# Loads ahead, stores issued by ACT, and a first chunk without a state, in a one-core hybrid decoder layer

## The chip, the core and the metric

The kernel runs on one core of a Trainium2 chip, in one launch. The metric is the device time of an execution in microseconds (us), as the median of several runs. The core has five engines that each work through their own list of instructions in order and wait for one another by semaphores: PE (TensorE, matrix multiplies), DVE (VectorE, elementwise), ACT (ScalarE, activations, copies and casts), POOL (GpSimd) and SP (SyncE, which here issues every DMA). SBUF is the on-chip memory with 128 partitions, PSUM holds the results of matmuls in banks of 128 x 512 float32, and DRAM is the memory outside. A tile is a buffer in SBUF or PSUM. A tile pool gives each tag a fixed number of buffers, and a tile that needs a buffer waits until its last user is done. The names of engines with a q behind them (SPq) are their DMA issues.

## The reference

One decoder layer over 2048 tokens of width 1024, in float32. A normalised input goes through one projection into two head groups. Group A is a Mamba-2 scan over 16 heads of 64 in chunks of 128 tokens, with a causal convolution ahead and a gated norm behind. Group B is a short gated convolution. Both are put side by side, projected back, normalised and added; a gated embedding follows. Cut to what matters here:

```python
def ssd_chunked(x, dt, a, b_mat, c_mat, d_skip):
    ...
    a_cs = jnp.cumsum(adt, axis=-1)
    decay_in = jnp.exp(segsum(adt))
    cb = jnp.einsum("bclgn,bcsgn->bgcls", cc, bc)
    y_diag = jnp.einsum("bgrcls,bcsgrp->bclgrp", cb[:, :, None] * decay_in, xd)
    ...
    states = jnp.einsum("bclgn,bclgrp->bcgrpn", bc, xd * decay_states[..., None])
    init = jnp.zeros_like(states[:, :1])
    states = jnp.concatenate([init, states], axis=1)
    ...
    y_off = jnp.einsum("bclgn,bcgrpn->bclgrp", cc, prev_states) * decay_out[..., None]
    y = (y_diag + y_off).reshape(bsz, length, SSD_HEADS, p)
    return y + d_skip[:, None] * x

def hybrid_layer(...):
    h = rmsnorm(x, norm_pre)
    proj = h @ w_in
    ...
    y_ssd = ssd_chunked(xs, dt, a, bm, cm, d_skip).reshape(bsz, length, D_MIX_SSD)
    yz = (y_ssd * jax.nn.silu(z_ssd)).reshape(bsz, length, SSD_GROUPS, D_MIX_SSD // SSD_GROUPS)
    y_ssd = rmsnorm(yz, ssd_norm.reshape(SSD_GROUPS, -1)).reshape(bsz, length, D_MIX_SSD)
    v = causal_dwconv(sc_c * sc_h, sc_conv_w)
    y_sc = sc_b * v * jax.nn.silu(z_sc)
    mix = jnp.concatenate([y_ssd, y_sc], axis=-1) @ w_out
    x = x + rmsnorm(mix, norm_post)
    gate = jax.nn.sigmoid(x @ w_ple_gate)
    return x + gate * (p_i @ w_ple_proj)
```

## The kernel before

The layout is transposed: features lie on the partitions, tokens run along the row. Tokens come in two halves of 1024 (index b) and four groups of 512 (index tg). Each big matrix product is made from float32 operands that were split into a high and a low part: ACT casts the high part, DVE subtracts to get the low part, and PE runs three passes (`PASSES`, L219). `split_w` (L145) does this for weights, `split_act` (L212) for activations. Weights come from one list through six buffers (`Weights`, L118); a weight is loaded and split, or it was split before, stored in DRAM and is loaded ready (`stored`, L152).

Stage A is the input projection. It takes both halves one after the other, with a Winograd-like scheme of seven products in place of eight (`Wino`). Products of column groups `gc`, `gb` (short convolution), `xs`, `z`, `cb` (scan) follow `order_` (L347). During the second half `later_weights` (L537) splits weights of later stages between the products: first those of the embedding's gate (`loads`, `sg_d`), then the lower rows of the output projection, in sixteen pieces A_o that are loaded into four buffers (tag h2), split by `keep` and stored to `so_d`. The results of stage A (xs_d, gz_d, cb_d, acs_d, ysc_d) go to DRAM.

The heads' stage puts two works side by side on PE. `under` (L894) multiplies the short convolution's part of the output projection (matmuls os, 256 units of three passes); each bank is copied by ACT to po (L918) and stored to part_d by SP (L919). Between the units runs the scan as a list of steps: for each half b four pairs j of head groups. PE's order is fixed as it is written (`InOrder`, L807). The other engines' order is made by the compiler's scheduler, which simulates the program and lets instructions run ahead of the written order. In a pair, `loads` brings xs, `mask_load` the four rows m from acs_d (four buffers), `transposes` makes xd and xdd, `decays` and `mask` run the exponentials on ACT (L1003, L1040) and the masks on DVE (L1043). `states` multiplies (pst), walks the chunks on DVE (L1027, into sprev, with the last state kept in carry for the next half) and scales ea (L1030). `offsets` multiplies the state of each chunk with ea (py from ea and sprev), `outputs` adds the inner products (py from m and xd), then DVE forms the rows (L1071, L1072), SP stores them to yz_d (L1073), ACT squares them (L1075, L1077) and DVE sums the squares (L1078, ssum). After the four pairs `inv_rms` (L236) makes the norm: PE sums over partitions (pn), ACT copies, SP stores to and loads from grs_d, ACT and DVE make the inverse root.

Normalised rows for the output projection are made by `mixes` (L883): `mix_load` loads pairs of rows into the three buffers of pool pld (class `Loads`, L832), `mix_pair` scales (L872) and splits them. The unit counter in `under` takes one entry of the list `new` per unit, in the first half only at every second unit.

Stage three, `out_proj` (L1155), multiplies the heads' part of the output projection (mo, L226) and adds the stored partial sums part (L1180) into tiles x (tag x2, 36 buffers), with ACT's squares behind; `norm` and `residual` add the input xres (L1210, L1213). `gate_seven` (L1240) multiplies for the gate (mg). The pool pl3 holds the loads of part and xres in three buffers. `second(tg, ..., lag)` (L1293) says how many units ahead the residual's loads begin. The pools of this stage take the memory of the heads' pools t4 and per, so a tile there waits for the last user of what lay there.

Of the kernel before, what the change touches and what calls it, by code (L numbers as in the profile page):

```python
# [7 lines left out]
F32 = mybir.dt.float32  # L8
# [56 lines left out]
def hybrid_kernel(ctx: ExitStack, tc: tile.TileContext, xT, pT, w_t, w_dt, w_o, w_g, w_p, cols_d, cst_d, outT):  # L65
# [303 lines left out]
    with ExitStack() as st:  # L369
# [167 lines left out]
        def later_weights():  # L537
# [24 lines left out]
            for d in range(KD):  # L562
                for q in range(2):
                    w = A.ph.tile([P, TG], F32, tag="h2", name=f"A_o{d}_{q}")
                    nc.sync.dma_start(w.rearrange("p (k c) -> p k c", c=P), w_o[d, :, 4 * (q + 2):4 * (q + 2) + 4, :])
                    keep(so_d[d][q], w, f"A_os{d}_{q}")
                    yield
# [314 lines left out]
    L = Loads(ctx, "pld", 3)  # L882
    def mixes(tg, k0):  # L883
# [5 lines left out]
    with ExitStack() as st:  # L889
        t4 = st.enter_context(tc.tile_pool(name="t4", bufs=2))  # L890
        per = st.enter_context(tc.tile_pool(name="per", bufs=1))
        carry = per.tile([P, 4, P], F32, name="carry")

        def under():  # L894


            new, unit = [], 0
# [40 lines left out]
        def heads(b):  # L938
# [3 lines left out]
            def begin():  # L942
                s["ct"] = per.tile([P, TB], F32, tag="ct", name=f"ct_{b}")
# [3 lines left out]
                s["gsb"] = [per.tile([P, TB], F32, tag=f"gsb{gr}", name=f"gsb_{b}{gr}") for gr in range(2)]  # L947
                s["btok"] = per.tile([P, NCH, P], F32, tag="btok", name=f"btok_{b}")
# [24 lines left out]
            def pair(j):  # L973
# [35 lines left out]
                def states():  # L1009
# [5 lines left out]
                    sp_ = st["sp"] = t4.tile([P, NCH, P], F32, tag="sprev", name=f"sprev_{b}{j}", bufs=1)  # L1015
                    ea = st["ea"]
                    if b == 0:
                        G.memset(sp_[:, 0, :], 0.0)
                    else:
                        G.tensor_copy(sp_[:, 0, :], carry[:, j, :])  # L1020
                    for c in range(NCH):
                        if c == NCH - 1 and b == NB - 1:
                            break
                        dstn = sp_[:, c + 1, :] if c + 1 < NCH else carry[:, j, :]
                        for hh in range(2):
                            hs = slice(64 * hh, 64 * hh + 64)
                            V.scalar_tensor_tensor(dstn[:, hs], sp_[:, c, hs], ea[:, hh, (c + 1) * CH - 1:(c + 1) * CH],  # L1027
# [17 lines left out]
                def offsets():  # L1045
# [3 lines left out]
                    for c in range(NCH):  # L1049
# [349 lines left out]
```

## Time and profile before

| What | us |
|---|---|
| median of 3 runs | 1663.52 |
| lowest and highest run | 1659.56, 1663.94 |
| profiled execution | 1660.71 |
| its span, first to last instruction | 1659.0 |
| DVE busy | 1273.4 |
| ACT busy | 805.7 |
| POOL busy | 69.3 |

The profile is of one execution. Its span is the time from the first to the last instruction; 1.7 us of the execution lie outside it. Busy time of an engine leaves out its semaphore and DMA-issuing instructions. Stage A ends at about 1031 us, the heads' stage at about 1306 us, the output projection at about 1496 us of the span. In a time line a row gives the start and the length in us, engine, line, operation, the tile written and the tiles read, the shape and how many instructions were merged; in square brackets stand the idle time ahead of it and what ended it.

### The profile page before, as it was taken

The page shows a single profiled execution, that of the slowest core. Times are in us where ns is not written, and L with a number is a line of the kernel's source. Part 1 is how long each engine was busy: PE and PEld are TensorE (multiplying, and loading weights), DVE is VectorE, ACT ScalarE, POOL GpSimd, SP SyncE. Part 2 cuts the span into 40 slices and gives each one's busy share as a digit, 9 for nine tenths or more (in the row PEclk, how much of TensorE's full clock was granted, in tenths as well). Part 3 has the DMA queues.
Part 4 walks back from the last instruction along what each step waited for, and adds up shares of the span by engine and source line. Part 5 has one row for each costly group of instructions (what it writes and reads, how often), then busy time and mean ns, then how long its engine had stood idle before and what let it go on. Part 6 is the DMA issues. An engine that isn't in the chain of part 4 may idle for free.

```text
span 1659.0 us, 22821 instructions
## 1 busy us (share of the span) xinstructions
PE 1634.0 (98%) x8296; PEld 1344.2 (81%) x8296; DVE 1273.4 (77%) x1913; ACT 805.7 (49%) x1450; POOL 69.3 (4%) x79
## 2 busy tenths in 40 slices
PE   9999999999999999999999999999999999999998
PEld 8888888888888888788888888888788788888776
DVE  6998777987769999877768678478777747687785
ACT  8663444434337555543435345466667424234342
POOL 0000000000000311000000001000100000000000
PEclk9999999999999999999999999999999999999999
DMA  9352322774216478951323227788788635547996
GB/s 324 140 197 83 101 94 82 258 242 142 72 64 219 178 269 283 298 172 64 108 64 107 71 66 266 254 303 292 278 288 293 202 113 180 160 160 253 323 309 218
DMA packets 135557, 314.73 MB, mean 190 GB/s; under 512 B 18698, under 2 KB 20234, under 8 KB 135444
## 3 DMA queue, kind: packets, MB, share of 16 engines
q1 hardware_dynamic: 135444, 313.27, 55.3%
q8 instruction: 65, 1.06, 0.3%
q14 instruction: 48, 0.39, 0.1%
HBM read 221.81 MB, written 91.41 MB: 189 GB/s over the span
## 4 chain that ended last, share of the span: by engine, by line
PE 74%; DVE 10%; DMA 9%; ACT 4%; issue 2%; SPq 0%; DVEq 0%; ACTq 0%
PE mo L226 10%; PE mg_X L1278 4%; PE mg_Y L1278 4%; PE os L817 3%; PE A_ple L226 2%; DMA m<-acs_d 2%; ACT m L1040 1%; PE A_xs1X L322 1%; PE A_gc6X L322 1%; PE A_gb7X L322 1%; PE A_gb5X L322 1%; PE A_gc7X L322 1%; PE A_z3X L322 1%; PE A_xs3X L322 1%; PE A_gb6X L322 1%
## 5 line engine op out<-in xcount | busy, mean ns | idle before, releaser
L817 PE MATMUL os<-act_m,ws_os 128*128 128x512 f32 x768 | 184.6, 397 | 0.7 <-ACT A_z L749 0.7
L226 PE MATMUL mo<-act_m,ws_o 128*128 128x512 f32 x768 | 179.3, 394 | 3.5 <-DVE x L1180 3.3
L226 PEld LDWEIGHTS mo<-act_m,ws_o 128*128 128x128 f32 x768 | 144.0, 189 | 37.8 <-DVE x L1180 6.0
L817 PEld LDWEIGHTS os<-act_m,ws_os 128*128 128x128 f32 x768 | 142.9, 189 | 34.6 <-issue 4.2
L1278 PE MATMUL mg_X<-act_x2s,ws_g 128*128 128x512 f32 x384 | 90.8, 393 | 0.7 <-ACT gth L1249 0.7
L147 DVE TENSOR_TENSOR ws_A_gb<-wr_A_gb,ws_A_gb 128x512 fp32r<-128x512 f32 x96 | 65.7, 684 | 27.1 <-ACT ws_A_gb L146 27.1
L1278 PEld LDWEIGHTS mg_X<-act_x2s,ws_g 128*128 128x128 f32 x384 | 70.8, 188 | 18.6 <-ACT gth L1249 1.7
L146 ACT CAST ws_A_gc<-wr_A_gc 128x512 fp32r<-128x512 f32 x96 | 59.7, 622 | 49.7 <-PE A_gc5X L322 8.3
L146 ACT CAST ws_A_gb<-wr_A_gb 128x512 fp32r<-128x512 f32 x96 | 59.7, 622 | 48.4 <-issue 5.0
L668 DVE SCALAR_TENSOR_TENSOR xo<-ux,cols,xo 128x1024 f32<-128x1024 f32 x60 | 76.6, 1280 | 5.3 <-ACT xo L664 4.2
L1040 ACT ACTIVATE m<-m,adt 128x128 f32<-128x128 f32 x256 | 79.8, 390 | 0.5
L147 DVE TENSOR_TENSOR ws_A_gc<-wr_A_gc,ws_A_gc 128x512 fp32r<-128x512 f32 x96 | 65.8, 685 | 12.2 <-ACT ws_A_gc L146 11.4
L1278 PE MATMUL mg_Y<-act_x2s,ws_g 128*128 128x512 f32 x288 | 68.1, 392 | 1.7 <-DVE kp L1251 1.2
L1278 PEld LDWEIGHTS mg_Y<-act_x2s,ws_g 128*128 128x128 f32 x288 | 53.5, 188 | 14.7 <-DVE kp L1251 2.4
L1043 DVE SCALAR_TENSOR_TENSOR m<-m,gsb 128x1024 f32<-128x1024 f32 x32 | 39.5, 1247 | 28.2 <-ACT m L1040 20.0
L1180 DVE TENSOR_TENSOR x<-mo,part 128x512 f32<-128x512 f32 x32 | 22.1, 689 | 47.4 <-PE mo L226 42.4
L1185 ACT ACTIVATE sq<-x 128x512 f32<-128x512 f32 x28 | 17.7, 633 | 70.5 <-DVE x L1180 70.4
L146 ACT CAST ws_A_z<-wr_A_z 128x512 fp32r<-128x512 f32 x48 | 29.9, 623 | 40.9 <-DVE wr_A_z L199 13.9
L215 ACT CAST act_m<-mraw 128x512 fp32r<-128x512 f32 x64 | 37.5, 620 | 23.8 <-DMA mraw<-ysc_d 9.6
L146 ACT CAST ws_A_xs<-wr_A_xs 128x512 fp32r<-128x512 f32 x48 | 29.9, 623 | 36.6 <-issue 11.6
L226 PE MATMUL A_ple<-act_p,ws_p 128*128 128x512 f32 x192 | 45.8, 396 | 0.1
L147 DVE TENSOR_TENSOR ws_A_z<-wr_A_z,ws_A_z 128x512 fp32r<-128x512 f32 x48 | 32.9, 685 | 16.6 <-ACT ws_A_z L146 16.5
(521 smaller groups left out, 3742.7 us busy)
## 6 DMA issues: line engine op xcount, KB each, us to landing
ws_g<-sg_d SPq DMA_DIRECT2D x56, 512.0 KB, 5.0
wr_A_gc<-in_w_t_dram SPq DMA_DIRECT2D x64, 256.0 KB, 2.7
wr_A_gb<-in_w_t_dram SPq DMA_DIRECT2D x64, 256.0 KB, 3.0
ws_os<-so_d SPq DMA_DIRECT2D x32, 512.0 KB, 5.7
m<-acs_d SPq DMA_DIRECT2D x32, 512.0 KB, 6.4
sg_d<-A_gs SPq DMA_DIRECT2D x28, 512.0 KB, 4.3
ple_d<-A_pe SPq DMA_DIRECT2D x32, 256.0 KB, 3.9
wr_A_xs<-in_w_t_dram SPq DMA_DIRECT2D x32, 256.0 KB, 3.0
```

Of the source, the lines that this page charges most:

```text
L146: S.copy(sp[:, 0, :kn, :], raw[:, :kn, :])
L147: V.tensor_tensor(sp[:, 1, :kn, :], raw[:, :kn, :], sp[:, 0, :kn, :].bitcast(F32), ALU.subtract)
L215: S.copy(a[:, 0, :], src)
L226: TE.matmul(out, sp[:, a, (k0 + k) % 4, :], act[k0 + k][:, b, :], start=k0 + k == 0 and q == 0, stop=k0 + k == n - 1 and q == 2)
L322: TE.matmul(out, sp[:, a, k % 4, :], t[:, b, ts_], start=p in OPENS and k == 0 and q == 0, stop=k == nk - 1 and q == 2, skip_group_check=True)
L668: V.scalar_tensor_tensor(o, u[:, q:q + TB], col(w0 + q), o, ALU.mult, ALU.add)
L817: inst = f(*a, **k)
L1040: S.activation(m[:, c, :], m[:, c, :], AF.Exp, bias=nacs[b][:, h, c:c + 1])
L1043: V.scalar_tensor_tensor(mf, mf, 1.0, s["gsb"][gr], ALU.min, ALU.mult)
L1180: evac.append(V.tensor_tensor(x2[d], ps[:, i, :], pt[:, i, :], ALU.add))
L1185: S.activation(sq, x2[d], AF.Square)
L1278: TE.matmul(out, sp[:, a, k, :], ops_[t, p][k][:, b, :], start=p in OPENS and m_ == 0, stop=m_ == 11, skip_group_check=True)
```

## The change

- Stored halves: the sixteen pieces A_o are loaded three ahead of the piece that is split, in the written order. The four buffers stay.
- Rows ahead: for token group 2 the eight raw tiles of the short convolution are loaded one by one into pool praw (`load_raw`), from the last quarter of the first two groups' units on, and split one by one (`mix_tile`). The loads for groups 3 and 0 through pld are written earlier, and their splits are spread with empty entries (`no`).
- Stores: part_d and yz_d are stored by ACT (`S.dma_start`), the first right behind ACT's copy to po, the second behind ACT's square of the same tile.
- First chunk: the state ahead of chunk 0 is no longer cleared or copied into sprev by POOL. In the first half, chunk 0 has no product with a state, and chunk 1's state is a copy of pst. In the second half carry is read directly.
- Memory: ct, gsb and btok move to a new pool pg between t4 and per. In stage three the x tiles get a pool px of their own, then comes pl3, then the rest (pp).
- Residual loads for groups 2 and 3 begin 3 and 4 units ahead, in place of 2.

```diff
+            ahead = []
+            for n in range(2 * KD + 3):
+                if n < 2 * KD:
+                    d, q = divmod(n, 2)
+                    ahead.append(A.ph.tile([P, TG], F32, tag="h2", name=f"A_o{d}_{q}"))
+                    nc.sync.dma_start(ahead[n].rearrange("p (k c) -> p k c", c=P),
+                                      w_o[d, :, 4 * (q + 2):4 * (q + 2) + 4, :])
+                if n >= 3:
+                    d, q = divmod(n - 3, 2)
+                    keep(so_d[d][q], ahead[n - 3], f"A_os{d}_{q}")
                     yield
...
+    def mix_tile(raws, tg, k):
+        acts_o[tg][KD + k] = split_act(raws.pop(k), f"m_{tg}_{KD + k}", FIRST[2 * (tg % 2) + k // 4])
...
         t4 = st.enter_context(tc.tile_pool(name="t4", bufs=2))
+        pg_ = st.enter_context(tc.tile_pool(name="pg", bufs=1))
         per = st.enter_context(tc.tile_pool(name="per", bufs=1))
...
+            def load_raw(tg, k):
+                t = praw.tile([P, 4, P], F32, tag="wraw", name=f"mraw_{tg}_{KD + k}").rearrange("p k c -> p (k c)")
+                b, o = divmod(tg * TG, TB)
+                nc.sync.dma_start(t, ysc_d[b][k, :, o:o + TG])
+                raws[k] = t
...
+                    if dp == KD - 2:
+                        if t == 0:
+                            new += [lambda k=k: load_raw(2, k) for k in range(KD)]
+                        else:
+                            new += [no] * 10 + [lambda: mix_load(L, 0, 0), lambda: mix_load(L, 0, 2)]
...
                             S.copy(o, ps)
-                            nc.sync.dma_start(part_d[tg][dp + di], o)
+                            S.dma_start(part_d[tg][dp + di], o)
                         if dp == KD - 2 and tg < NG - 1:
-                            new += mixes(*((tg + 2, KD) if tg + 2 < NG else (tg + 2 - NG, 0)))
+                            ...
+                            if tg == 0:
+                                for k in range(KD):
+                                    new.append(lambda k=k: mix_tile(raws, 2, k))
+                                    if k in (2, 4, 6):
+                                        ld(3, KD + k - 2)()
+                            elif tg == 1:
+                                new += [mx(3, KD), ld(3, KD + 6), no, mx(3, KD + 2), no, mx(3, KD + 4), no, no, mx(3, KD + 6)]
+                            else:
+                                new += [mx(0, 0), ld(0, 4), no, mx(0, 2), ld(0, 6), no, no, no, mx(0, 4), no, no, mx(0, 6)]
...
-                    if b == 0:
-                        G.memset(sp_[:, 0, :], 0.0)
-                    else:
-                        G.tensor_copy(sp_[:, 0, :], carry[:, j, :])
+                    prev = st["prev"] = [carry[:, j, :] if b else None] + [sp_[:, c, :] for c in range(1, NCH)]
                     for c in range(NCH):
...
+                        if prev[c] is None:
+                            V.tensor_copy(dstn, pst[:, :P])
+                            continue
...
-                    for c in range(NCH):
+                    for c in range(0 if b else 1, NCH):
...
-                    nc.sync.dma_start(yz_d[b][jt], yv)
                     if j == 0:
                         S.activation(ssum, yv, AF.Square)
                     else:
                         S.activation(sq, yv, AF.Square)
                         V.tensor_tensor(ssum, ssum, sq, ALU.add)
+                    S.dma_start(yz_d[b][jt], yv)
...
+        px = st.enter_context(tc.tile_pool(name="px", bufs=NG * KD + 4))
+        L3 = Loads(st, "pl3", 3)
         pp = st.enter_context(tc.tile_pool(name="pp", bufs=2))
-        L3 = Loads(st, "pl3", 3)
...
-        second(2, 32, (40, 41, 43, 44), 2)
+        second(2, 32, (40, 41, 43, 44), 3)
...
-        second(3, 36, (56, 58, 60, 61), 2)
+        second(3, 36, (56, 58, 60, 61), 4)
```

More of the change, by code (lines that the diff above doesn't have):

```diff
@@ L561, in later_weights @@
                     yield
[L562 to L566, printed above, removed]
+            ahead = []
[8 more added lines that the diff above has]
+                    keep(so_d[d][q], ahead[n - 3], f"A_os{d}_{q}")
                     yield
@@ L890, in hybrid_kernel @@
         t4 = st.enter_context(tc.tile_pool(name="t4", bufs=2))
+        pg_ = st.enter_context(tc.tile_pool(name="pg", bufs=1))
         per = st.enter_context(tc.tile_pool(name="per", bufs=1))
         carry = per.tile([P, 4, P], F32, name="carry")
+        no = lambda: None
         def under():
-            new, unit = [], 0
+            new, unit, raws = [], 0, {}
+            def load_raw(tg, k):
[3 more added lines that the diff above has]
+                raws[k] = t
             for t in range(0, NG, 2):
@@ L942, in begin @@
             def begin():
-                s["ct"] = per.tile([P, TB], F32, tag="ct", name=f"ct_{b}")
+                s["ct"] = pg_.tile([P, TB], F32, tag="ct", name=f"ct_{b}")
                 nc.sync.dma_start(s["ct"], cb_d[b][0])
@@ L946, in begin @@
                 nc.sync.dma_start(s["bt"], cb_d[b][1])
-                s["gsb"] = [per.tile([P, TB], F32, tag=f"gsb{gr}", name=f"gsb_{b}{gr}") for gr in range(2)]
-                s["btok"] = per.tile([P, NCH, P], F32, tag="btok", name=f"btok_{b}")
+                s["gsb"] = [pg_.tile([P, TB], F32, tag=f"gsb{gr}", name=f"gsb_{b}{gr}") for gr in range(2)]
+                s["btok"] = pg_.tile([P, NCH, P], F32, tag="btok", name=f"btok_{b}")
                 s["ssum"] = [per.tile([P, TB], F32, tag=f"ssum{gr}", name=f"ssum_{b}{gr}") for gr in range(2)]
@@ L1014, in states @@
                                       s["btok"][:, c, 64 * gr:64 * gr + 64], xdd[gr][:, c, :], start=True, stop=True)
-                    sp_ = st["sp"] = t4.tile([P, NCH, P], F32, tag="sprev", name=f"sprev_{b}{j}", bufs=1)
+                    sp_ = t4.tile([P, NCH, P], F32, tag="sprev", name=f"sprev_{b}{j}", bufs=1)
                     ea = st["ea"]
-                    if b == 0:
-                        G.memset(sp_[:, 0, :], 0.0)
-                    else:
-                        G.tensor_copy(sp_[:, 0, :], carry[:, j, :])
+                    prev = st["prev"] = [carry[:, j, :] if b else None] + [sp_[:, c, :] for c in range(1, NCH)]
                     for c in range(NCH):
@@ L1023, in states @@
                             break
-                        dstn = sp_[:, c + 1, :] if c + 1 < NCH else carry[:, j, :]
+                        dstn = prev[c + 1] if c + 1 < NCH else carry[:, j, :]
+                        if prev[c] is None:
+                            V.tensor_copy(dstn, pst[:, :P])
+                            continue
                         for hh in range(2):
                             hs = slice(64 * hh, 64 * hh + 64)
-                            V.scalar_tensor_tensor(dstn[:, hs], sp_[:, c, hs], ea[:, hh, (c + 1) * CH - 1:(c + 1) * CH],
+                            V.scalar_tensor_tensor(dstn[:, hs], prev[c][:, hs], ea[:, hh, (c + 1) * CH - 1:(c + 1) * CH],
                                                    pst[:, c * P + 64 * hh:c * P + 64 * hh + 64], ALU.mult, ALU.add)
@@ L1056, in offsets @@
                                 bank[gr, c // 4, hh] = open_bank(f, TE.matmul(
-                                    st["py"][gr][hs, cs], st["sp"][rows, c, hs], st["ea"][rows, hh, cs], start=f is None,
+                                    st["py"][gr][hs, cs], st["prev"][c][rows, hs], st["ea"][rows, hh, cs], start=f is None,
                                     stop=False, skip_group_check=True))
@@ L1178, in out_proj @@
                     del sp[d]
-                x2[d] = pp.tile([P, TG], F32, tag="x2", name=f"x2_{tg}_{d}", bufs=NG * KD + 4)
+                x2[d] = px.tile([P, TG], F32, tag="x2", name=f"x2_{tg}_{d}")
                 evac.append(V.tensor_tensor(x2[d], ps[:, i, :], pt[:, i, :], ALU.add))
@@ L1215, in tmp @@
         def tmp(name):
-            return pp.tile([P, TG], F32, tag="x2", name=name, bufs=NG * KD + 4)
+            return px.tile([P, TG], F32, tag="x2", name=name)
         ops_, sums_ = {}, {}
```

3 lines of the change are left out of this document (2 added, 1 removed).

## The prediction

> **What bounds the kernel now.** I read the page first, then the waits of the tensor engine (PE), then the time lines of all engines around each of those waits.
>
> ```profile
> span 1659.0 us, 22821 instructions
> PE 1634.0 (98%) x8296; PEld 1344.2 (81%) x8296; DVE 1273.4 (77%) x1913; ACT 805.7 (49%) x1450; POOL 69.3 (4%) x79
> ```
>
> PE is busy for 1634.0 of 1659.0 us, and no other engine is over 81%. The kernel is bound by PE, so an edit can win only where PE waits, where PE's clock is lower, or where it takes matmuls away. The view of PE's waits says where that is (PE line, releaser, us in total, times, longest):
>
> ```profile
> PE A_cb0Z L322 <- ACT A_cb L326: 3.6, 1, 3.6
> PE mo L226 <- DVE x L1180: 3.3, 1, 3.3
> PE py L817 <- DVE ea L1030: 3.2, 5, 0.8
> PE pn L817 <- DVE ssum L1078: 2.7, 2, 2.3
> PE mg_Y L1278 <- DVE kp L1251: 1.2, 1, 1.2
> ...
> PE pg L817 <- DMA bt<-cb_d: 1.1, 1, 1.1
> ...
> PE mg_Y L1278 <- DVE x L1213: 0.5, 1, 0.5
> ```
>
> These seven come to 15.6 us, and the edits touch the neighbourhood of each. The clock adds something. In the view by windows the columns are busy us of each engine, then the granted PE clock, the DMA share and GB/s:
>
> ```profile
> 700.00:720.00 20.00, 16.43 (x73) 13.29 (x72) 17.18 (x29) 8.56 (x18) 3.88 (x5) 1.00 0.84 279
> 1160.00:1180.00 20.00, 17.31 (x120) 12.76 (x116) 18.02 (x20) 12.23 (x22) 3.61 (x1) 0.91 0.87 319
> 1300.00:1320.00 20.00, 16.67 (x75) 12.59 (x74) 15.23 (x25) 11.84 (x22) 0.00 (x0) 0.97 0.56 187
> 1320.00:1340.00 20.00, 20.00 (x83) 15.94 (x83) 8.66 (x13) 3.92 (x7) 0.00 (x0) 0.94 0.66 211
> ```
>
> Behind the wait for ssum the clock is 0.91 over 20 us, which is 0.09 x 20 = 1.8 us. Behind the wait for x it is 0.97 and 0.94, which is 0.6 + 1.2 = 1.8 us. What can be won at all is therefore 15.6 + 3.6 = 19.2 us and the matmuls that go.
>
> **The turn into the last stage (pools px, pl3, pp).** Before, the buffers of pl3 lie where ssum lay, so the first load of a partial sum has to wait until ssum has been read. Time lines of SP, DVE and PE:
>
> ```profile
> 1284.41 2.35 DVE L1043 SCALAR_TENSOR_TENSOR m<-m,gsb 128x1024 f32<-128x1024 f32 x2
> ...
> 1308.30 1.12 SPq L246 DMA_DIRECT2D grs_d<-ssum  x4
> ...
> 1313.19 0.32 SPq L249 DMA_DIRECT2D pn_q<-grs_d  x1
> 1313.61 0.37 SPq L856 DMA_DIRECT2D part<-part_d  x1
> ...
> 1311.94 1.89 DVE L147 TENSOR_TENSOR ws_o<-wr_o,ws_o 128x512 fp32r<-128x512 f32 x3
> 1318.45 0.69 DVE L1180 TENSOR_TENSOR x<-mo,part 128x512 f32<-128x512 f32 x1 [4.62 <-DMA part<-part_d]
> ...
> 1306.40 9.46 PE L226 MATMUL mo<-act_m,ws_o 128*128 128x512 f32 x41
> 1319.19 1.22 PE L226 MATMUL mo<-act_m,ws_o 128*128 128x512 f32 x2 [3.33 <-DVE x L1180]
> ```
>
> The pools of the stage before take 72 KB a partition in t4 (by the shapes in the code: po 4, gz 8, xs 16, m 16, xd 8, xdd 8, ea 8, sprev 4), and the 36 tiles of px take exactly 72 KB. So pl3 comes to lie on the new pool pg (ct, gsb, btok), whose last reader here is the mask step L1043 of the last pair, over at 1286.8. The load no longer has to wait for ssum. DVE is free at 1311.94 + 1.89 = 1313.8 and would end L1180 at 1314.5, while PE runs out of work at 1306.40 + 9.46 = 1315.9. The wait of 3.3 us goes, and I take the 1.8 us of clock behind it with it: **5.1 us**. Next late is DVE itself, with 1.4 us to spare. If the load keeps its place in SP's line behind pn_q, nothing goes: bounds 0 and 5.1.
>
> **The norm between the two halves (rows loaded ahead).** For token group 2 the eight raw tiles are now loaded into praw during the units before, in place of pairs through the three buffers of pld.
>
> ```profile
> 1159.94 3.90 SPq L856 DMA_DIRECT2D mraw<-ysc_d  x3
> ...
> 1165.21 1.14 ACT L215 CAST act_m<-mraw 128x512 fp32r<-128x512 f32 x2 [5.95 <-DMA mraw<-ysc_d]
> ...
> 1165.87 0.69 DVE L216 TENSOR_TENSOR act_m<-mraw,act_m 128x512 fp32r<-128x512 f32 x1 [1.22 <-ACT act_m L215]
> ...
> 1171.02 1.05 PE L817 MATMUL pn<-ssum,ones_d 128*32 128x512 f32 x4 [0.35 <-DVE ssum L1078]
> 1174.41 1.05 PE L817 MATMUL pn<-ssum,ones_d 128*32 128x512 f32 x4 [2.33 <-DVE ssum L1078]
> 1175.39 4.60 PE L817 MATMUL os<-act_m,ws_os 128*128 128x512 f32 x12
> 1181.10 2.06 PE L817 MATMUL pg<-ct,bt 64*128 64x128 f32 x32 [1.11 <-DMA bt<-cb_d]
> ```
>
> ACT stood 5.95 us for a raw tile, DVE stood behind ACT for 1.22 us and then did a split (0.69 us) ahead of its next step towards ssum, L1072, and PE's norm matmuls waited for that. With the tiles there, the casts run in ACT's empty 5.95 us, and DVE's 1.22 + 0.69 = 1.9 us go from the chain to ssum; the other splits that stand between the two ssum steps go ahead as well. I take both waits (2.7 us) and the clock behind them (1.8 us): **4.5 us**, bounds 1.9 and 4.5. The wait of pg for bt (1.1 us) stays in part, because PE comes there earlier while the load goes out earlier as well: **0.5 us**, bounds 0 and 1.1.
>
> The Trainium skill, page "TensorE: Matmul & The Clock Gate", section "What's actually happening", has the clock halved only after an idle window of about 3.4 us. The trace differs both ways: 3.57 us idle at 706 us left 1.00, and gaps of at most 2.33 us at 1174 gave 0.91. By that rule the second 1.8 us would not go with the gap, and the time would be 1649.4 instead of 1647.6; I go by the rows.
>
> **Stores issued by ACT.** 32 stores of po and 16 of yz leave SP. In the pair at 1078 us:
>
> ```profile
> 1074.35 3.71 PE L817 MATMUL py<-m,xd 128*64 128x128 f32 x64
> ...
> 1078.96 0.32 SPq L1073 DMA_DIRECT2D yz_d<-xs  x1
> ...
> 1082.18 1.59 SPq L1035 DMA_DIRECT2D m<-acs_d  x2
> ...
> 1088.63 1.06 ACT L1003 ACTIVATE ea<-m 64x1024 f32<-64x1024 f32 x1 [1.01 <-DMA m<-acs_d]
> ...
> 1098.70 0.46 DVE L1027 SCALAR_TENSOR_TENSOR carry<-sprev,ea,pst 128x64 f32<-128x64 f32 x2
> 1099.09 2.35 DVE L1030 SCALAR_TENSOR_TENSOR ea<-ct,ea 128x1024 f32<-128x1024 f32 x2
> ...
> 1101.49 1.76 PE L817 MATMUL py<-ea,sprev 64*64 64x128 f32 x56 [0.61 <-DVE ea L1030]
> ```
>
> The buffers m are free when py ends (1074.35 + 3.71 = 1078.1), yet the last two loads go out at 1082.18, behind two yz stores that wait for DVE. Without the stores they go out up to 4 us earlier, and ACT's wait of 1.01 us goes; ACT's chain of exponentials is what ea, and so PE, waits for. Against that, about four issues a pair now stand on ACT ahead of the masks. The trace has no DMA issue on ACT. Below, one costs nothing, if ACT's datapath works on while its sequencer issues; the yz store needs no further wait, because the square before it waited for the same tile. Above, I take SP's rows: 0.32 us alone, 1.59 / 2 = 0.80 us in a busy queue. Between these ends I take the nearest row, 0.32: 4 x 0.32 = 1.3 us lost against 1.0 + 0.2 (a scan step less, below) won. **Net 0**, bounds +3.2 us won (the whole wait for ea) and 8 pairs x 4 x 0.80 = 25.6 us lost. PE waited for ea five times in the eight pairs, so there is little cover.
>
> The Trainium skill, page "DMA: Bandwidth & Descriptors", section "Issuing engines are not separate DMA queues", says that another issuing engine saves only the sequencer's issue time. The rows above speak against it here: the loads were late by a wait in SP's line, not by 0.32 us of issue. By that rule the bt gain would be nothing and the sum 0.5 us smaller.
>
> **First chunk of the scan.** For the first half, 16 matmuls on a zero state go, two scan steps become one copy (0.46 / 2 = 0.2 us a pair), and POOL's clears and copies go.
>
> ```profile
> L817 PE MATMUL py<-ea,sprev 64*64 64x128 f32 x512 | 18.1, 273 | 3.5 <-DVE ea L1030 3.2
> ```
>
> 18.1 us / 512 = 35 ns each, and 16 of them are **0.6 us**. The bounds are 0 and 0.6.
>
> **Stored halves loaded ahead.**
>
> ```profile
> 689.95 5.27 SPq L544 DMA_DIRECT2D so_d<-A_os  x4
> ...
> 697.32 1.37 SPq L565 DMA_DIRECT2D A_o<-in_w_o_dram  x3
> ...
> 703.23 1.35 ACT L542 CAST A_os<-A_o 128x512 fp32r<-128x512 f32 x2 [3.21 <-DMA A_o<-in_w_o_dram]
> ```
>
> ACT stood 3.21 us for A_o, so A_cb came late and PE waited 3.6 us. The loads went out at 697.32, behind four stores that took 5.27 us to leave SP. Three loads ahead in program order they can go between those stores, about 5 us earlier. But there are four buffers before and after, so a load still waits for the cast four tiles back, and the DMA share in that window is 0.84. Bounds 0 and 3.6; I take half, **1.8 us**.
>
> **Residual loads 3 and 4 units ahead.** The waits behind them (kp L1251 1.2 and x L1213 0.5 us) come from the fourth load of a group, which needs the buffer of the first. Only its place in SP's line can improve: **0.6 us**, bounds 0 and 1.7.
>
> **Sum.** 5.1 + 4.5 + 0.5 + 0 + 0.6 + 1.8 + 0.6 = 13.1 us from 1660.71 us, the profiled execution's own time: 1647.6, **1648 us**. The median shown is 1663.52, 2.8 us above that execution, and the runs lie between 1659.56 and 1663.94; that spread goes into the range.
>
> **The rivals.**
> - One of the two large waits stays: the first partial load is still issued behind pn_q, or the casts of group 2 still stand ahead of ssum. For it: SP, ACT and DVE work strictly in line, and every edit reorders the lines. Against: the reason for the late load, the shared memory, is taken away. 1647.6 + 5.1 = 1652.7, or 1647.6 + 4.5 = 1652.1 us.
> - ACT's issues eat the gain: 0.32 us each, four a pair, eight pairs = 10.2 us, with nothing won back by earlier m loads: 1657.8 us, within 0.3% of before. Two large waits that both stay give 1657.2 and go with it.
> - Slower: ACT's issues cost as much as SP's in a busy queue, 0.80 us. 25.6 us lost on the way to ea against 13.1 won: 1673 us. It decides from 13.1 / 32 = 0.41 us an issue. For it: the DMA share was 0.87 in the window of 1160 us, and PE's waits for ea leave little cover. Against: ACT has idle time ahead of the squares, in which earlier loads can start the masks (35.3 us over 12 squares):
>
> ```profile
> L1077 ACT ACTIVATE gz<-xs 128x1024 f32<-128x1024 f32 x12 | 12.7, 1055 | 35.3 <-DVE xs L1072 35.3
> ```
>
>
> **How the numbers follow.** Forecast 0.57, one wait stays 0.18, eaten 0.14, slower 0.11. A difference of 0.3% (5 us) is about what a measurement of this kernel can tell from no change. Faster: 0.57 + 0.18 less a little for run spread, 0.74; same 0.15; slower 0.11. The low end is all waits and clocks gone, 1660.7 - 19.2 - 0.6 = 1641, less 1.2 of spread: 1639. The high end is the eaten case, 1657.8, with 3.2 of spread: 1661.
>
> **What would show it.** Right: PE's waits without x L1180 and ssum L1078, clock 1.00 in the windows behind them, part issued before the norm's stores, casts of group 2 with no DMA wait, m loads right behind the end of py. Wrong: a longer wait for ea, gaps on ACT at its DMA issues, or a new wait of PE for act_m in the last stage because the splits moved.

## The result, and the profile after

| | us |
|---|---|
| before, median | 1663.05 (1659.56 to 1663.94) |
| after, median of 4 runs | 1654.62 (1653.93 to 1655.4) |
| ratio | 0.994, 95% interval 0.9917 to 0.9963 |
| profiled execution of after, its span | 1654.73, 1653.0 |

The kernel became faster, by 8.4 us between the medians and by 6.0 us between the two profiled executions (1660.71 to 1654.73). The prediction said 1648, so about half of the forecast gain of 13.1 us came (6.0 us between the profiles). To see where, I cut each span at three points of PE's time line: the first matmul of os, of mo and of mg.

| us | stage A | heads | output projection | gate |
|---|---|---|---|---|
| before | 1033.0 | 273.5 | 179.9 | 172.6 |
| after | 1040.0 | 263.8 | 176.5 | 172.7 |

The heads' stage won 9.6 us, the output projection 3.5, and stage A gave 7.0 of these 13.1 us back. The waits of PE in the kernel after (line, releaser, us in total, times, longest):

```profile
PE A_cb0X L322 <- ACT A_cb L326: 7.2, 1, 7.2
PE pn L822 <- DVE ssum L1111: 2.2, 2, 1.2
PE mg_Y L1312 <- DMA ws_g<-sg_d: 1.7, 1, 1.7
PE mo L226 <- DVE x L1214: 1.6, 2, 1.4
```

The wait for A_cb has doubled, from 3.6 to 7.2 us. The wait of py for ea (3.2 us) and that of pg for bt (1.1 us) are gone. The wait for ssum is hardly smaller (2.7 to 2.2), the one for x is halved (3.3 to 1.6). The windows of after (busy us of PE, PEld, DVE, ACT, POOL, then the granted clock, the DMA share, GB/s):

```profile
700.00:720.00 20.00, 12.75 (x51) 10.11 (x50) 14.56 (x24) 8.11 (x19) 3.87 (x5) 0.83 0.84 295
1160.00:1180.00 20.00, 17.34 (x177) 13.03 (x176) 17.35 (x20) 10.95 (x21) 0.00 (x0) 1.00 0.97 339
1300.00:1320.00 20.00, 18.59 (x85) 14.15 (x84) 12.71 (x23) 10.02 (x19) 0.00 (x0) 1.00 0.40 124
1320.00:1340.00 20.00, 20.00 (x88) 16.11 (x88) 9.56 (x15) 4.25 (x7) 0.00 (x0) 1.00 0.45 147
```

The clock behind ssum and behind x is whole again (0.91, 0.97 and 0.94 before), as predicted. Behind A_cb it fell from 1.00 to 0.83. Not all of these 0.17 x 20 = 3.4 us are lost: cut finer, the clock is 0.50 from 705.27 to 712.10, and PE stood until 709.09 anyway. Twelve matmuls behind the wait took 4.41 us in place of 2.88, which is 1.5 us. The clock is 0.50 once more from 275.19 to 278.60, where before has 1.00; twelve matmuls there took 4.61 us, in before 3.03. With the longer wait (3.6 us) these make 6.7 of the 7.0 us that stage A lost.

What the stores did is seen in the pair whose rows were shown of before. Time line of SP in after:

```profile
1082.90 2.54 SPq L1069 DMA_DIRECT2D m<-acs_d  x4
1085.54 2.74 SPq L1040 DMA_DIRECT2D gz<-gz_d  x2
```

All four loads of m go out in one row, with no store between; before, three stores stood between the second and the third. The last is out at 1085.44, 0.8 us behind the end of py (1080.91 + 3.71 = 1084.62); before it was 5.7 us (1083.77 against 1078.06). Time line of ACT in after, the same pair:

```profile
1085.53 1.06 ACT L1108 ACTIVATE ssum<-xs 128x1024 f32<-128x1024 f32 x1 [10.37 <-DVE xs L1106]
1085.53 0.36 ACTq L1112 DMA_DIRECT2D yz_d<-xs  x1
...
1088.94 0.57 ACT L941 COPY po<-os 128x512 f32<-128x512 f32 x1
1089.40 1.06 ACT L1036 ACTIVATE ea<-m 64x1024 f32<-64x1024 f32 x1
1089.54 0.33 ACTq L942 DMA_DIRECT2D part_d<-po  x1
1090.36 1.05 ACT L1036 ACTIVATE ea<-m 64x1024 f32<-64x1024 f32 x1
```

The issue of yz runs beside the square, the issue of part beside the next exponential, and the instruction behind begins with no idle time ahead of it. In these rows an issue of 0.33 to 0.36 us costs ACT's line nothing.

### The profile page after: what moved, and what is told of

Its sections match the earlier page's. It is cut to its first block, busy times and chain, and to the rows that moved or that the text cites. A ratio compares the mean times of both kernels' runs of the same rounds, so it can differ in the third digit from the quotient of the medians.

```text
span 1653.0 us, 22708 instructions
## 1 busy us (share of the span) xinstructions
PE 1631.0 (99%) x8264; PEld 1342.3 (81%) x8264; DVE 1273.0 (77%) x1909; ACT 805.6 (49%) x1450; POOL 58.8 (4%) x71
## 4 chain that ended last, share of the span: by engine, by line
PE 81%; DVE 9%; DMA 6%; issue 2%; ACT 1%; SPq 0%; ACTq 0%; DVEq 0%
PE mo L226 10%; PE os L822 8%; PE mg_X L1312 5%; PE mg_Y L1312 4%; PE py L822 2%; PE A_ple L226 2%; DMA A_o<-in_w_o_dram 2%; PE A_xs1X L322 1%; PE A_gc6X L322 1%; PE A_gb7X L322 1%; PE A_gb5X L322 1%; PE A_z1X L322 1%; PE A_gc7X L322 1%; PE A_z3X L322 1%; PE A_xs3X L322 1%
## 5 line engine op out<-in xcount | busy, mean ns | idle before, releaser
L147 DVE TENSOR_TENSOR ws_A_gb<-wr_A_gb,ws_A_gb 128x512 fp32r<-128x512 f32 x96 | 65.9, 687 | 26.2 <-ACT ws_A_gb L146 26.2
L147 DVE TENSOR_TENSOR ws_A_gc<-wr_A_gc,ws_A_gc 128x512 fp32r<-128x512 f32 x96 | 66.0, 687 | 12.3 <-ACT ws_A_gc L146 11.4
L147 DVE TENSOR_TENSOR ws_A_z<-wr_A_z,ws_A_z 128x512 fp32r<-128x512 f32 x48 | 32.9, 686 | 17.6 <-ACT ws_A_z L146 17.5
```

The source lines that it names most:

```text
L147: V.tensor_tensor(sp[:, 1, :kn, :], raw[:, :kn, :], sp[:, 0, :kn, :].bitcast(F32), ALU.subtract)
```

## The experiments

All ratios are against the kernel before on the same chip, with the 95% interval. The stages of the profiled execution of each, in us:

| kernel | median | ratio | A | heads | out | gate |
|---|---|---|---|---|---|---|
| e1, stored halves loaded as before | 1651.09 | 0.9913 [0.9898, 0.9928] | 1037.3 | 263.0 | 179.9 | 172.1 |
| e2, both stores on SP | 1668.9 | 1.0018 [1.0008, 1.0029] | 1038.2 | 275.6 | 180.0 | 172.5 |
| e3, rows as before | 1660.58 | 0.9962 [0.9948, 0.9976] | 1042.0 | 267.9 | 177.9 | 171.7 |
| e4, pools as before | 1652.33 | 0.9917 [0.9903, 0.9932] | 1039.1 | 264.1 | 174.7 | 171.2 |
| e7, before with ACT's stores alone | 1652.06 | 0.993 [0.991, 0.9949] | 1036.5 | 265.4 | 174.7 | 172.9 |
| e8, before with the new pools alone | 1661.92 | 0.9996 [0.998, 1.0011] | 1034.6 | 274.3 | 178.2 | 173.0 |
| e9, stored halves and pools as before | 1647.77 | 0.9902 [0.9885, 0.992] | 1036.8 | 264.4 | 175.1 | 172.5 |
| e12, pools as before, casts pinned | 1643.46 | 0.9879 [0.9861, 0.9898] | 1031.0 | 263.3 | 174.7 | 172.4 |
| e10, po's stores on SP | 1660.78 | 0.9956 [0.9938, 0.9974] | 1040.6 | 266.5 | 179.5 | 172.4 |
| e11, yz's stores on SP | 1664.24 | 0.9983 [0.9971, 0.9996] | 1038.4 | 270.4 | 180.0 | 172.4 |
| e13, e12 with rows as before | 1646.31 | 0.9869 [0.9846, 0.9892] | 1031.9 | 266.8 | 174.8 | 171.6 |
| e14, e12 with two issues for each po | 1653.66 | 0.9914 [0.9895, 0.9933] | 1029.7 | 269.8 | 179.8 | 171.9 |

**Undoing one part at a time.**

e1, the loads of the stored halves back in their old place:

```diff
-            ahead = []
-            for n in range(2 * KD + 3):
-                ...
+            for d in range(KD):
+                for q in range(2):
+                    w = A.ph.tile([P, TG], F32, tag="h2", name=f"A_o{d}_{q}")
+                    nc.sync.dma_start(w.rearrange("p (k c) -> p k c", c=P), w_o[d, :, 4 * (q + 2):4 * (q + 2) + 4, :])
+                    keep(so_d[d][q], w, f"A_os{d}_{q}")
```

> The changed kernel with the stored halves A_o loaded as before (one ahead of its split). In the changed kernel PE waits 7.2 us for A_cb at 702 us and loses 1.4 us of clock behind it; before it was 3.6 us and none. Theory: loading ahead moved ACT's casts of A_o ahead of the copy of A_cb, so a late load holds the copy. Then PE's wait for A_cb comes back to about 3.6 us at clock 1.00, stage A ends some 5 us earlier, about 1649.5 us. Rival: the loads are late because the DMA queues are full there, whatever the order; then the wait stays over 6 us and the time about 1654.6 us.

The wait for A_cb fell to 3.4 us and stage A got 2.7 us shorter, not 5: the clock over 700 to 720 us stayed at 0.83, where the theory had 1.00. The ratio's interval overlaps that of after, so the time alone doesn't settle it; stage A over all kernels does. With the loads in the old place it is 1033.0 to 1037.3 us (before, e1, e7, e8, e9), with the loads ahead 1038.2 to 1042.0 (after, e2, e3, e4, e10, e11): 4.1 us between the means. Loading ahead lost time.

e2, both stores back on SP:

```diff
-                            S.dma_start(part_d[tg][dp + di], o)
+                            nc.sync.dma_start(part_d[tg][dp + di], o)
...
+                    nc.sync.dma_start(yz_d[b][jt], yv)
...
-                    S.dma_start(yz_d[b][jt], yv)
```

> The changed kernel with all 48 stores (po and yz) issued by SP again, yz right behind L1072. Theory: the stores in SP's line made the m loads late, and that was PE's wait for ea; then PE's waits for ea come back (3 us or more), the last two m loads of a pair stand behind the yz stores again, and the time is about 1658 us. Rival: ACT pays for the issues, and the waits for ea went by the shorter first chunk and the other order; then the time is the same or lower, 1650 to 1654.6 us.

Its median is 2.6 us above that of before: without ACT's stores the rest of the change, taken together, wins nothing. Its waits of PE:

```profile
PE py L822 <- DVE ea L1064: 6.2, 9, 2.1
PE mo L226 <- DVE x L1214: 3.8, 2, 3.3
PE px L822 <- DVE xs L1105: 1.9, 1, 1.9
```

py waits for ea nine times, 6.2 us. The last two loads of m stand behind the yz stores again (the second yz at 1086.92, m at 1087.33), as the theory has it. The heads' stage is at 275.6 us, 11.8 longer than in after. The loss is larger than either theory said.

e3, the rows as before (the edit is the diff's part on `under`, taken back):

```diff
-                    if dp == KD - 2:
-                        if t == 0:
-                            new += [lambda k=k: load_raw(2, k) for k in range(KD)]
-                        ...
...
-                            ld = lambda tg, k: lambda: mix_load(L, tg, k)
-                            ...
+                            new += mixes(*((tg + 2, KD) if tg + 2 < NG else (tg + 2 - NG, 0)))
```

> The changed kernel with the rows for groups 2, 3 and 0 loaded and split as before (pairs through pld). Theory: loading the raw tiles ahead is what shortened PE's wait for ssum from 2.7 us at clock 0.91 to 2.2 us at clock 1.00; then the wait and the clock come back, 2 to 4 us, about 1657.5 us. Rival: the norm is held by the exponentials and squares on ACT either way; then the wait for ssum stays near 2.2 us and the time near 1654.6 us.

The heads' stage is 4.1 us longer than in after, as the theory has it, though the wait for ssum is not where it shows: that is 2.1 us here and 2.2 in after. What returned are waits of py for m and for ea (1.8 and 0.6 us) and a clock of 0.98 and 0.94 in the windows of 1160 and 1180 us.

e4, the pools of before (px, pg and the order of pl3 taken back):

```diff
-        pg_ = st.enter_context(tc.tile_pool(name="pg", bufs=1))
...
-        px = st.enter_context(tc.tile_pool(name="px", bufs=NG * KD + 4))
-        L3 = Loads(st, "pl3", 3)
         pp = st.enter_context(tc.tile_pool(name="pp", bufs=2))
+        L3 = Loads(st, "pl3", 3)
```

> The changed kernel with the pools of before (no pg, no px; pl3 behind pp, so on ssum). Theory: the place of pl3 was the reason for the wait for x; then the first load of part goes out behind the norm's stores again, PE's wait for x L1214 grows from 1.6 us by 2 to 3 us and the clock behind it falls, about 1658 us. Rival: SP, freed of the stores, issues that load early enough either way; then the time stays near 1654.6 us.

The theory falls. With the old pools the output projection is 1.8 us shorter than in after, and the time line shows no wait for x at the turn. Time lines of SP, PE and DVE in e4:

```profile
1304.71 1.12 SPq L246 DMA_DIRECT2D grs_d<-ssum  x4
1306.86 0.35 SPq L249 DMA_DIRECT2D pn_q<-grs_d  x1
1307.38 1.60 SPq L861 DMA_DIRECT2D part<-part_d  x3
...
1303.15 19.17 PE L226 MATMUL mo<-act_m,ws_o 128*128 128x512 f32 x83
...
1311.65 0.68 DVE L1212 TENSOR_TENSOR x<-mo,part 128x512 f32<-128x512 f32 x1
```

and of after:

```profile
1284.30 0.38 SPq L861 DMA_DIRECT2D part<-part_d  x1
...
1303.82 7.64 PE L226 MATMUL mo<-act_m,ws_o 128*128 128x512 f32 x33
1312.87 9.37 PE L226 MATMUL mo<-act_m,ws_o 128*128 128x512 f32 x40 [1.41 <-DVE x L1214]
...
1304.90 4.90 DVE L216 TENSOR_TENSOR act_m<-mraw,act_m 128x512 fp32r<-128x512 f32 x8
1309.72 2.50 DVE L147 TENSOR_TENSOR ws_o<-wr_o,ws_o 128x512 fp32r<-128x512 f32 x4
1312.13 0.69 DVE L1214 TENSOR_TENSOR x<-mo,part 128x512 f32<-128x512 f32 x1
```

The new pools do what they say: part is loaded 23 us earlier (1284.30 against 1307.38). But the step for x runs at the same place of DVE's line in both, right behind twelve splits that end at about 1312. What differs is PE's line, which the compiler's scheduler writes in this stage from its own simulation. With part early, it puts the matmuls that need x behind 33 others; with part late, behind 41 (in before and in e14, where PE stands there; e4 has no gap that would show its own number). In after PE gets to them 8 matmuls or 9.46 - 7.64 = 1.8 us sooner, and stands. With 41 it would get there in e4 at 1303.15 + 9.46 = 1312.6, and the step for x is over at 1312.3.

**One part alone on the kernel before, and two undone.**

e7, the two store edits alone, on the kernel before:

```diff
-                            nc.sync.dma_start(part_d[tg][dp + di], o)
+                            S.dma_start(part_d[tg][dp + di], o)
...
-                    nc.sync.dma_start(yz_d[b][jt], yv)
...
+                    S.dma_start(yz_d[b][jt], yv)
```

> The kernel before, with the two kinds of stores issued by ACT and nothing else changed. Theory A (the stores stood in SP's line ahead of the loads of m, xs and part; putting them on SP again cost the kernel after about 13 us): most of the gain comes without any other part, 9 to 13 us less than the kernel before, ratio 0.992 to 0.9945, and PE's wait for ea (3.2 us before) is gone. Theory B (the stores are only in the way once the rows are loaded ahead through SP as well): 3 us less or nothing, ratio 0.998 to 1.0, the wait for ea stays over 1.5 us.

Theory A holds in its time: 11.7 us less than before, by ratio as much as the whole change. Its condition on ea doesn't: PE's wait for ea is not gone, but 1.4 us in place of 3.2; that for ssum is 1.1 (2.7 before), that for x 0.2 (3.3 before). PE's line has the same order of tiles as in the kernel before, so only the times of what it waits for moved. SP in e7, at the turn:

```profile
1302.82 1.12 SPq L246 DMA_DIRECT2D grs_d<-ssum  x4
1304.86 0.35 SPq L249 DMA_DIRECT2D pn_q<-grs_d  x1
1305.37 1.40 SPq L856 DMA_DIRECT2D part<-part_d  x3
```

SP in before, the two rows that the prediction left out between the norm's store (1308.30) and pn_q (1313.19):

```profile
1309.82 0.34 SPq L919 DMA_DIRECT2D part_d<-po  x1
1312.65 0.36 SPq L142 DMA_DIRECT2D wr_o<-in_w_o_dram  x1
```

The norm's load pn_q went out 4.9 us behind the norm's store, and the load of part right behind it, because a load of wr_o stood ahead of them. A buffer of wr_o comes free with a split on DVE. The first split of that block (L147) began at 1311.94, and the load went out 0.71 us later, as it ended; in e8 and e14, where the load of wr_o stands in the same place, the distance is 0.71 us as well. In e7 it stands behind part, and pn_q follows the norm's store after 2.0 us. So the wait for x in before came from a load in SP's line that waited for DVE. The shared memory can't be what cost the 3.3 us: with the same pools the wait of mo for x is 0.2 us in e7. No run moves that load of wr_o alone; the account rests on these rows and on e14, below, where the load stands ahead of pn_q again and the wait is back.

e8, the new pools alone, on the kernel before:

```diff
+        pg_ = st.enter_context(tc.tile_pool(name="pg", bufs=1))
...
-        pp = st.enter_context(tc.tile_pool(name="pp", bufs=2))
+        px = st.enter_context(tc.tile_pool(name="px", bufs=NG * KD + 4))
         L3 = Loads(st, "pl3", 3)
+        pp = st.enter_context(tc.tile_pool(name="pp", bufs=2))
```

> The kernel before, with the new pools pg, px and pl3 and nothing else. Theory of the prediction (the first load of part waits for ssum's memory): the load goes out before the norm's stores, PE's wait for x (3.3 us) goes, 3 to 5 us less, ratio 0.997 to 0.998. Rival (the x step waits in DVE's line behind splits, and the order of the schedule, not the memory, decides; in the kernel after the old pools were 2 to 4 us better): the wait for x stays at 2 us or more, ratio 0.999 to 1.002.

The rival holds. The load of part went out at 1289.28, and PE still waited 2.7 us, now for DVE's line. PE, then DVE in e8:

```profile
1308.85 6.51 PE L226 MATMUL mo<-act_m,ws_o 128*128 128x512 f32 x28
1318.07 6.20 PE L226 MATMUL mo<-act_m,ws_o 128*128 128x512 f32 x26 [2.71 <-DVE x L1182]
...
1315.53 1.89 DVE L147 TENSOR_TENSOR ws_o<-wr_o,ws_o 128x512 fp32r<-128x512 f32 x3
1317.33 0.68 DVE L1182 TENSOR_TENSOR x<-mo,part 128x512 f32<-128x512 f32 x1
```

Here PE has 28 matmuls ahead of the wait.

e9, the edits of e1 and e4 together:

> The kernel after, with the stored halves loaded as before and the old pools. Theory A (the two parts lose in places of their own, about 0.0027 and 0.0023 of the time): the gains add up, ratio 0.988 to 0.990, about 1646 us on a chip where the kernel before takes 1663; waits for A_cb about 3.5 us and for x about 0.3. Theory B (each of the two only shook the schedule into a luckier order): no better than either one alone, 0.991 to 0.994.

The ratio lies at the edge between the two theories, with an interval that reaches into both. Stage A is as short as in e1 and the output projection as in e4, which speaks for A, but the wait for ssum was 2.8 us in this run, and the time doesn't decide it.

e12, the old pools, and every cast of `later_weights` held behind the copies that are written ahead of it:

```diff
+    copied, pin = [], lambda cast: copied and tc.add_manual_dep(cast.ins, copied[-1].ins.name, NOSYNC, reason="written order")
...
-                        S.copy(keep[pr, p], out)
+                        copied.append(S.copy(keep[pr, p], out))
...
-                S.copy(t[:, 0, :], src)
+                pin(S.copy(t[:, 0, :], src))
```

> The kernel after with the old pools, and with every cast of later_weights held behind the copies of stage A that are written before it; PE's order is the same. Theory A (PE's wait for A_cb, 7.2 us in the kernel after, is ACT standing at a cast that the schedule moved ahead of A_cb's copy): that wait goes, with the clock behind it, stage A is 6 to 9 us shorter than with the old pools alone, ratio 0.986 to 0.988. Rival (the casts held back use up the buffers, pile up at the end of stage A and delay weights or rows there): the wait moves, ratio 0.991 to 0.995.

Theory A holds: the wait for A_cb is gone and stage A is 8.1 us shorter than in e4. Time line of ACT in after, where the wait arises:

```profile
702.43 0.60 ACT L542 CAST A_os<-A_o 128x512 fp32r<-128x512 f32 x1
...
703.94 0.63 ACT L704 ACTIVATE th<-A_z 128x512 f32<-128x512 f32 x1
707.93 0.62 ACT L542 CAST A_os<-A_o 128x512 fp32r<-128x512 f32 x1 [3.37 <-DMA A_o<-in_w_o_dram]
708.46 0.58 ACT L326 COPY A_cb<-A_cb0X 128x512 f32<-128x512 f32 x1
```

and in e12:

```profile
697.41 0.64 ACT L704 ACTIVATE th<-A_z 128x512 f32<-128x512 f32 x1
699.13 0.59 ACT L326 COPY A_cb<-A_cb0X 128x512 f32<-128x512 f32 x1 [1.08 <-PE A_cb0X L322]
```

In after, two casts of stored halves stand ahead of the copy that PE waits for, the second 3.37 us for its data. An earlier one, at 696.57, had already stood 2.89 us. The scheduler had moved them far ahead of their written place. In e12 the copy runs as soon as PE has made its bank. Window of e12:

```profile
700.00:720.00 20.00, 20.00 (x89) 16.55 (x89) 15.51 (x24) 8.25 (x17) 2.87 (x3) 1.00 0.23 77
```

PE is busy throughout at clock 1.00. With 1643.46 us it has the lowest median of all kernels here, under both before and after (the ratio of e13, below, can't be told from its own); its four runs lie within 0.5 us.

**Which store, what the rows are worth, what an issue costs.**

e10 puts po's stores back on SP, e11 yz's:

```diff
-                            S.dma_start(part_d[tg][dp + di], o)
+                            nc.sync.dma_start(part_d[tg][dp + di], o)
```

```diff
+                    nc.sync.dma_start(yz_d[b][jt], yv)
...
-                    S.dma_start(yz_d[b][jt], yv)
```

> The kernel after, with the 32 stores of po back on SP and the 16 of yz left on ACT. Both kinds back on SP cost about 13 us (ratio 1.0018 against 0.994). Theory A (the yz stores, which wait for DVE's row step, hold the loads of m and xs): po alone costs little, ratio 0.994 to 0.9965, the wait for ea stays under 1 us. Theory B (the po stores, which wait for PE's bank and ACT's copy all through the stage, hold them): ratio 0.999 to 1.002, the wait for ea is 3 us or more. Theory C (each holds some): 0.997 to 0.999.

> The kernel after, with the 16 stores of yz back on SP and the 32 of po left on ACT. Theory A (the yz stores hold the loads of m): most of the 13 us come back, ratio 0.999 to 1.002, the wait for ea is 3 us or more. Theory B (the po stores do): ratio 0.994 to 0.9965, the wait for ea stays under 1 us. Theory C (each some): 0.997 to 0.999.

The ratio of e10 is as theory A has it, that of e11 as theory C. Against after the heads' stage is 2.7 us longer with po's stores on SP, 6.6 us with yz's, 11.8 with both (263.8, 266.5, 270.4, 275.6). Both kinds hold SP's line; the 16 of yz more than the 32 of po, and both together lose more than the two one by one. Theory A's condition on ea fails in both: the wait is 2.3 and 2.2 us. The output projection is 3.0 and 3.5 us longer too: at the turn PE waits 3.1 and 3.5 us for x, behind 29 and 28 matmuls in place of 33, so a part of the loss goes with the order that the scheduler wrote there.

e13 is e12 with the edit of e3:

> The kernel with the old pools and the pinned casts (0.9879), with the rows loaded and split as before. Theory of the prediction (rows ahead are worth 4.5 us: 2.7 us of PE's wait for ssum and 1.8 us of clock): ratio 0.990 to 0.991, the heads' stage 3 to 5 us longer, the wait for ssum back at 2.5 us or more. Rival (with the stores out of SP's line the rows come in time anyway, as in the run with ACT's stores alone, where the wait for ssum was 1.1 us): ratio 0.987 to 0.989.

The heads' stage is 3.5 us longer than in e12, as the prediction's theory has it, but the wait for ssum is 2.3 us, under its bound. The ratio is on the rival's side. The two intervals, taken beside different runs of the kernel before, overlap for the most part. I read it with e3 as 3.5 to 4.1 us in the stage, seen in two profiles and not confirmed by the times.

e14 issues each store of po as two halves:

```diff
-                            S.dma_start(part_d[tg][dp + di], o)
+                            [S.dma_start(part_d[tg][dp + di][r:r + 64], o[r:r + 64]) for r in (0, 64)]
```

> The kernel with the old pools and the pinned casts (0.9879), with every store of po issued by ACT as two halves of 64 partitions: 32 more issues on ACT, the same bytes. Theory A (an issue runs beside ACT's datapath and costs its line nothing): ratio 0.987 to 0.989, the heads' stage within 1 us of 263.3. Rival (the prediction's choice, 0.32 us of ACT's line each, with PE close behind): up to 32 x 0.32 = 10 us more, ratio 0.991 to 0.994, and a wait for ea or m grows.

The ratio is the rival's, at its lower end. The heads' stage is 6.5 us longer than in e12, 0.20 us for each added issue. ACT in e14:

```profile
1136.28 4.29 ACTq L941 DMA_DIRECT2D part_d<-po  x2
1140.61 1.06 ACT L1035 ACTIVATE ea<-m 64x1024 f32<-64x1024 f32 x1 [3.28 <-DMA yz_d<-xs]
...
1144.50 0.62 ACT L215 CAST act_m<-mraw 128x512 fp32r<-128x512 f32 x1
1144.63 1.10 ACTq L941 DMA_DIRECT2D part_d<-po  x2
1145.77 1.14 ACT L215 CAST act_m<-mraw 128x512 fp32r<-128x512 f32 x2 [0.65 <-ACT act_m L215]
```

Two issues in a row take 1.10 us, only the first of which fits beside the cast: ACT's datapath stands 0.65 us. In the first place the second issue waited until a yz store had landed, 3.28 us. The experiment isn't clean, since halves were issued and the scheduler moved other things: the output projection is 5.2 us longer as well, with a load of wr_o ahead of pn_q again and a wait for x of 3.2 us.

## Why the prediction was right or wrong

The direction was right, and 1654.6 lies in the range, in part by luck: the term put at nothing brought the gain, and the largest term, by the stages, a loss. Of the sum, 4.5 + 0.5 + 0 + 0.6 = 5.6 us were for the heads' stage, which won 9.6; 5.1 for the output projection, which won 3.5; 1.8 for stage A, which lost 7.0. Errors of both signs cancel in part.

- **What bounds the kernel**: right. The gains and losses that the stages show are waits of PE or its clock, most of them at the places listed.
- **The turn into the last stage, 5.1 us**: the failed step is "Before, the buffers of pl3 lie where ssum lay, so the first load of a partial sum has to wait until ssum has been read", and with it the 1.4 us said to be to spare. e7 removes the wait with the old pools, and e8 moves the load and keeps the wait. By SP's rows the cause was a load of wr_o in SP's line. The row of PE's 41 matmuls was also taken as fixed, and the new pools themselves made it 33. The 5.1 us exist (e7, with the old pools, has an output projection 5.2 us shorter than before, and e4 too), but ACT's stores bring them, and the pools hand 1.8 back.
- **Stores issued by ACT, net 0**: the mechanism (loads of m late behind stores in SP's line) was right, and the size was far off: 11.7 us alone in e7, and 13 to 14 us lost with both stores on SP (e2 against after, 1668.9 - 1654.6 = 14.3 between medians taken beside different runs of before, 13.3 between the spans). The term was mis-sized twice. The price of 0.32 us an issue fell away where an issue stood alone, since it ran beside the datapath (the 48 stores are six a pair, of which the sum took four); and I counted the gain on the wait for ea in one pair, while the stores also held loads behind the waits for ssum, bt and x. The upper bound of the gain, 3.2 us, was too small for this reason. The rule of the Trainium skill on this (page "DMA: Bandwidth & Descriptors", section "Issuing engines are not separate DMA queues") has another issuing engine save the sequencer's issue time alone; e2's waits and e7's rows of SP show a gain made of waits in line instead.
- **Rows ahead, 4.5 us**: 3.5 to 4.1 us by the stages of e3 and e13. The clock came back as said, and the casts of group 2 wait for no load any more. The step "DVE's 1.22 + 0.69 = 1.9 us go from the chain to ssum" failed: ACT now stands for a load of m ahead of the squares, in place of a raw tile:

```profile
1171.34 1.06 ACT L1036 ACTIVATE ea<-m 64x1024 f32<-64x1024 f32 x1 [2.72 <-DMA m<-acs_d]
...
1173.07 1.05 ACT L1110 ACTIVATE gz<-xs 128x1024 f32<-128x1024 f32 x1
```

  The rule of the Trainium skill that the prediction weighed (page "TensorE: Matmul & The Clock Gate", section "What's actually happening") asks for an idle window of about 3.4 us. The rows decide against it here: in before the clock is 0.50 from 1175.60 to 1179.01, right behind the gap of 2.33 us, and in after, with gaps of 1.0 and 1.2 us, it stays at 1.00.
- **pg and bt, 0.5 us**: 1.1 us came. The wait is 0.6 us in e2 and not in the list of after or e7, so part of it belongs to the stores.
- **First chunk, 0.6 us**: not tried alone. PE's matmuls fell from 8296 to 8264, which is 32 and not 16, so at 35 ns it is an estimated 1.1 us: I counted the products in the code, and the trace has two records for each.
- **Stored halves ahead, 1.8 us won**: the sign was wrong. The step "Three loads ahead in program order they can go between those stores, about 5 us earlier" looked at SP alone. It left out that the scheduler moves the casts with the loads; in after they stand ahead of the copy that PE needs. Cost by stage A: 4.1 us on the mean. The wait of 3.6 us that was there to be won went with the pinned casts of e12, whose stage A is 2.0 us shorter than that of before; e12 has the half clock at 275 us as well, which before has not.
- **Residual loads, 0.6 us**: net 0. The waits for kp and x (1.2 + 0.5 us) are gone, and one of 1.7 us for ws_g stands in their place. Over all kernels the gate's stage is 172.6 to 173.0 us without the edit (before, e7, e8) and 171.2 to 172.7 with it, 0.7 us between the means, which is the size forecast but lies within what other edits move. It wasn't tried alone. SP of after:

```profile
1517.88 0.38 SPq L861 DMA_DIRECT2D xres<-in_xT_dram  x1
1518.36 7.29 SPq L154 DMA_DIRECT2D ws_g<-sg_d  x4
```

  xres stands ahead of four weight loads now; before, one of these went out ahead of it (1523.99, xres at 1524.41). That this order is what made PE wait for ws_g is not shown.
- **Rivals**: "One of the two large waits stays" came nearest, 1652.7 against 1654.6, but not by its mechanism: of both waits a part stayed (1.6 of 3.3 us for x, 2.2 of 2.7 for ssum), and the clock behind both came back. "ACT's issues eat the gain" and "slower" fall with e7. Of the signs of being right, part ahead of the norm's stores, the casts, the whole clock behind ssum and x and the loads of m at the end of py came; that the waits for x and ssum would be gone did not.

## What to carry to other kernels

In a queue that runs in order, a store that waits for its producer costs what stands behind it; list every row between the load that is late and the one ahead of it before naming memory as the cause. Give such a store to an engine that has just made or read the tile, one issue behind that instruction, so that the issue runs beside the next one; two in a row didn't fit in e14. Where a scheduler writes the lines, moving a load moves its consumers and the matmuls as well: look for what it puts ahead of the instruction that the bounding engine waits for, and pin that order.

## What the runs showed of the hardware

The clock behind a gap of PE isn't set by the gap's length alone. At the same place of stage A, twelve matmuls behind the gap, with the same code for stage A in all, in before:

```profile
706.20 3.01 PE L322 MATMUL A_cb0Z<-act_A,ws_A_cb 128*128 128x512 f32 x12 [3.57 <-ACT A_cb L326]
```

in e9:

```profile
707.46 5.49 PE L322 MATMUL A_cb0Z<-act_A,ws_A_cb 128*128 128x512 f32 x12 [3.69 <-ACT A_cb L326]
```

and e8:

```profile
706.43 4.38 PE L322 MATMUL A_cb0Z<-act_A,ws_A_cb 128*128 128x512 f32 x12 [2.96 <-ACT A_cb L326]
```

Gaps of 3.57, 3.69 and 2.96 us left 1.00, 0.83 and 0.91 over the window of 700 to 720 us. So the profiled execution of before was the best of its kind in stage A; the same code took 1.6 to 4.3 us longer to the heads' stage in e8, e7, e9 and e1.

Finer windows show what goes with it. In these traces the clock is 1.00 or 0.50, and it changes only at edges that lie whole steps of 3.413 us apart (in before, 1175.60, 1179.01, 1318.96 and 1322.37). Where the edges fall differs from execution to execution. Here are steps of PE cut at these edges (where the clock didn't change, the edges are counted on in steps of 3.413 us):

| profile | step, us | PE idle in it, us | clock of the next step |
|---|---|---|---|
| before | 701.15 to 704.56 | 1.93 | 1.00 |
| before | 704.56 to 707.97 | 1.64 | 1.00 |
| before | 1172.19 to 1175.60 | 2.22 | 0.50 |
| e9 | 702.73 to 706.14 | 2.37 | 0.50 |
| e8 | 702.55 to 705.97 | 2.49 | 0.50 |

The gap of 3.57 us in before fell onto two steps, and neither held enough of it. Over all fourteen profiles, away from the ends of the span, each of the 21 steps at full clock with 2.05 us of idle or more was followed by one at half clock, and none with 1.0 to 1.8 us of idle; around 1.9 us it went either way (1.91 and 1.93). The half step at 275 us in after, e12 and e13 has no idle ahead of it and stays unexplained. That the idle of a step sets the clock of the next is read off these rows; no run here varies it alone.

So two gaps of nearly the same length cost nothing in one execution (before) and 2.5 us of slower matmuls in another (5.49 against 3.01 in e9). This is not all of the spread between runs: e12 and e13 have no gap there, and e12's four runs lie within 0.5 us, e13's within 2.5.
